# Four pairs of k tiles in three more units of a Strassen-like matmul kernel, and results added to memory by DMA

## The chip, the cores and the metric

The kernel runs on one core of a Trainium2 chip. A core has a matrix engine (PE, with its weight load PEld), a vector engine (DVE), a scalar engine (ACT), a general engine (POOL) and an engine that here only issues loads (SP). Each works through its own list of instructions in order; semaphores make one wait for another. DMA queues move data beside them. The metric is the device time of one execution in microseconds (us), as the median of several; smaller is better.

## The reference

The input is one sequence of 256 tokens with 2048 channels in float32, and one layer of a residual network is computed:

```python
u = rms_norm(h, norm_mix_w)
z = u @ w_in                                  # 2048 x 11264
...
gate_a, gate_b = jnp.split(jax.nn.sigmoid(gates), 2, axis=-1)
merged = gate_a * (y_a @ w_branch_a) + gate_b * (y_b @ w_branch_b)
h = h + merged @ w_out
u = rms_norm(h, norm_mlp_w)
h = h + jnp.square(jax.nn.relu(u @ w_up)) @ w_down      # 2048 -> 8192 -> 2048
return rms_norm(h, norm_final_w)
```

y_a comes from a gated linear recurrence (8 heads) and y_b from banded attention (16 heads) over parts of z. The change concerns the last columns of `u @ w_in`, which are the two gates, and the last part of `@ w_down` together with the final norm.

## The kernel before, in words

**Products.** Each float32 operand is split into a high part (rounded to fp32r) and a low part (what is left), by an ACT cast and a DVE subtraction (`split`, L88 to L90). A product of one tile of 128 k rows is three matmuls: high by high, high by low, low by high (`mm3`, L142 to L145).

**Units.** From the second half of the first gate on, the work is cut into units (`gemm_s`, L718 to L888). A unit makes 256 tokens by 1024 columns from 16 k tiles: two token blocks m = 0, 1 by two column blocks n = 0, 1 of 512. Of its 16 k tiles, r pairs (k, k + 4) are treated as 2 by 2 blocks in the manner of Strassen and Winograd: seven products for eight, with sums of weight blocks (`add`, L740 to L742, on DVE), sums of activation blocks (S2, S4, S5 and S7, made by `combos`, L615 to L646) and four running sums in PSUM that take copies of each other (`copy`, L770 to L773, on ACT) and are combined there (`more`, L775 to L777, on DVE). The other k tiles are plain products (`plain`). A unit has 192 − 3r matmuls of 128x512. With r = 3 the third pair is in mixed tiles X and Y, whose 256 KB halves are loaded one by one, and the k tiles 3 and 7 in another mixed pair `r0_3`, `r1_3`; with r = 4 all loads are whole 512 KB tiles.

The products are named p1, p3, p5, p2, p6, p7, p4 in the order of work, with px, py, px2 for the mixed tiles, and the plain pairs r0_k and r1_k. Product p7 goes into the sum c21 after ACT has copied that sum out (u1); u2 is the copy after p7.

The units in order: ga2 (second half of the first gate), gb0 and gb2 (second gate), then eight plain products with the branch weights, wo0 and wo2 (w_out), and four quarters of the MLP. A quarter has two w_up units and two w_down units, which are named up00, up02, dn00, dn02 in quarter 0, and so on to dn30 and dn32. All have r = 3 but wo2 and one w_up unit (r = 2) and the w_down units of quarters 0 to 2 (r = 4).

The last plain pair of a unit's second column block, with the hand-over of its results, is kept back as a closure (`late`) and issued within the next unit by `flush` (L892): with r = 4 before p5 (L794 to L797), with r = 3 after p2 (L809).

**Results.** A unit calls `done` or `out_of` per result of 128x512. Gates go through a sigmoid on ACT. For w_down, `out_of` (L1015 to L1039) has two ways. In quarters 0 to 2, ACT copies the PSUM sum to a token tile y (L1020) and POOL issues a DMA that adds it to the residual tile h in SBUF (L1021). In the last quarter DVE adds the sum to h directly (`evict`, L714 to L716); then ACT squares the tile for the final norm (`ysq`, L1024) and DVE multiplies it by the norm's weights `wf` (L1026). When n = 3 is done, the norm is finished and the output is written.

**Activations of a quarter.** `turn` (L973 to L985) transposes squared ReLU results on PE, ACT copies the blocks needed for the sums, and ACT and DVE split them; `turns` (L990 to L996) calls `combos` on them. `pairs` (L988) is 3 in the last quarter and 4 in the others. With four pairs `combos` makes the fourth entry of its sums in tiles of their own, S5m and S2m. The sums for x (Sx) are made once, before the gates, with three entries.

**Buffers and order.** Weights pass through rings of buffers: raw 6 + 2, high parts 4 + 2, low parts 4 + 2 (`BUFS`, `buf`, `piece`, `parts`, L662 to L699). A load is issued when DVE's split has released its raw buffer. PSUM has six banks for sums (`ps_k`). Token tiles of 128x512 share 17 buffers. The order of instructions on each engine is set by a scheduler, which goes by the program's order and by the priority that `tc.high_priority` raises.

Of the kernel before, what the change touches and what calls it, by code (L numbers as in the profile page):

```python
# [8 lines left out]
F32 = mybir.dt.float32  # L9
# [7 lines left out]
P = 128  # L17
T = 256
NM = T // P
D = 2048  # L20
KD = D // P
FF = 8192
NC = 512
# [27 lines left out]
def tile_hybrid_block(  # L51
# [5 lines left out]
    nc = tc.nc  # L57
    x, out = x[0], out[0]
# [29 lines left out]
    def split(hi, lo, src, copy=None):  # L88
        (copy or nc.scalar.copy)(hi, src)  # L89
        nc.vector.tensor_tensor(lo, src, hi.bitcast(F32), op=ALU.subtract)  # L90
# [7 lines left out]
    def new_act(what):  # L98

        return apool.tile([P, 4, 2, T], F32R, name=f"act_{what}", tag="act")  # L100
# [49 lines left out]
    def gemm(lhs, w, n0, nkt, what, wide=False, between=None):  # L150

        acc = new_acc(what)
        for kt, wh, wl in weights(w, n0, nkt, NC, what, wide=wide):
            if between and between[0][0] == kt:
                between.pop(0)[1]()
            for m in range(NM):
                mm3(acc[:, m, :], *lhs_of(lhs, kt, m), wh, wl, kt == 0, kt == nkt - 1)
        return acc
# [33 lines left out]
    xT = [new_act(f"x{c}") for c in range(4)]  # L192
# [14 lines left out]
    done = [0, 0]  # L207
    for kt, n in zip(starts, steps):
        c, a = kt // 4, kt % 4
# [290 lines left out]
    a, sc, vs, gws, ends = [None] * 4, [[] for _ in range(4)], [None] * 2, [None] * 2, []  # L500
# [28 lines left out]
    tk = ctx.enter_context(tc.tile_pool(name="tokens", bufs=1, reuse_waits="tile"))  # L529
# [6 lines left out]
    TOK = 17  # L536
# [49 lines left out]
    for g in range(2):  # L586
        qT = [qk_chunk(C_AQ + g * NC + i * T, f"aq{g}{i}", rstd8_t, None if g or i else acc_q0) for i in range(2)]
        kT = [qk_chunk(C_AK + g * NC + i * T, f"ak{g}{i}", rstd_t) for i in range(2)]
        acc = gemm(xT, w_in_n, C_AV + g * NC, KD, f"av{g}")
# [7 lines left out]
        for pr in range(5):  # L597
            last = pts
# [5 lines left out]
    def token(what):  # L604
        return tk.tile([P, NC], F32, name=what, tag="t", bufs=TOK)


    def sigmoid(gate, acc, m):
        with tc.high_priority(offset=2000):
            nc.scalar.activation(gate, acc, AF.Sigmoid, scale=rstd[:, m:m + 1])  # L610
        return gate

    R = 3

    def combos(lhs, what, home, blocks=None, n=R):  # L615

        a = blocks
        if not a:
            a = []
            for m in range(NM):  # L620
                for j in range(2):
                    t = tk.tile([P, R, P], F32, name=f"a{m}{j}_{what}", tag="t", bufs=TOK)
                    x = lhs[j][:, :R, :, m * P:(m + 1) * P].bitcast(F32)
                    nc.vector.tensor_tensor(t, x[:, :, 0, :], x[:, :, 1, :], op=ALU.add)
                    a.append(t)
        a11, a12, a21, a22 = a
        s5 = a22
        nc.vector.tensor_tensor(s5, a21, a22, op=ALU.subtract)
        s7 = a21
        nc.vector.tensor_tensor(s7, a11, a21, op=ALU.subtract)  # L630
        s2 = a11
        nc.vector.tensor_tensor(s2, s5, a11, op=ALU.subtract)
        s4 = a12
        nc.vector.tensor_tensor(s4, a12, s2, op=ALU.add)
        made = {}
        for two in ((5, s5), (4, s4)), ((2, s2), (7, s7)):
            if n > R:
                more = tk.tile([P, 2, 2, P], F32R, name=f"S{two[0][0]}m_{what}", tag="t", bufs=TOK)
            for q, (i, s) in enumerate(two):
                t = (tk if home == "a" else xp).tile([P, R, 2, P], F32R, name=f"S{i}_{what}", tag=f"S{i}{home}", bufs=1)  # L640
                split(t[:, :, 0, :], t[:, :, 1, :], s[:, :R])
                made[i] = [[t[:, k, u, :] for u in range(2)] for k in range(R)]
                if n > R:
                    split(more[:, q, 0, :], more[:, q, 1, :], s[:, R])
                    made[i].append([more[:, q, u, :] for u in range(2)])
        return made  # L646

    Sx = combos(xT, "x", "a")
    ga, gb = [], []
    for n in range(2):  # L650
        acc = gemm(xT, w_in_t, C_GA + n * NC, KD, f"ga{n}", wide=True)
# [62 lines left out]
    def evict(dst, acc):  # L714
        with tc.high_priority(offset=2000):
            nc.vector.tensor_tensor(dst, acc, dst, op=ALU.add)  # L716
# [175 lines left out]
    def flush():  # L892

        while late:
            late.pop()()

    for gates, c, col, what, fresh in ((ga, 2, C_GA, "ga", True), (gb, 0, C_GB, "gb", True), (gb, 2, C_GB, "gb", False)):
        gates += [[None] * NM for _ in range(2)]

        def done(m, n, acc, gates=gates, c=c, what=what):  # L900
            gates[c + n][m] = sigmoid(token(f"gate_{what}{c + n}{m}"), acc, m)

        gemm_s(xT, Sx, w_in_t, col + c * NC, f"{what}{c}", done, fresh=fresh)
    flush()


# [9 lines left out]
    for n in range(4):  # L916
        for y, w, gate, what in ((ya, w_branch_a, ga[n], "ba"), (yb, w_branch_b, gb[n], "bb")):
            acc = gemm2(y, w, n * NC, 8, f"{what}{n}")
# [35 lines left out]
    for n0 in (0, 2):  # L954
        for n in (n0, n0 + 1):
            for m in range(NM):
                t = token(f"h1_{n}_{m}")
# [10 lines left out]
    for qd in range(NQ):  # L968
        last = qd == NQ - 1
        uT = []  # L970
        pend = []

        def turn(ahead=0):  # L973

            c, rs = pend.pop(0)
            uT.append(new_act(f"u{qd}{c}"))
            hi, lo = uT[-1][:, :, 0, :], uT[-1][:, :, 1, :]
            for m in range(NM):
                tp = transpose4(rs[m], f"u{qd}{c}{m}")
                if c < 2:  # L980
                    blocks[m, c] = tk.tile([P, pairs, P], F32, name=f"a{m}{c}_u{qd}", tag="t", bufs=TOK)
                    nc.scalar.copy(blocks[m, c], tp[:, :pairs])
                with tc.high_priority(offset=ahead):
                    split(hi[:, :, m * P:(m + 1) * P], lo[:, :, m * P:(m + 1) * P], tp)

        Su = {}
        blocks = {}
        pairs = R if last else 4  # L988

        def turns():  # L990
            if len(hT) == 2:
                h_blocks(2)
            while pend:
                turn()
            if len(uT) == 2:
                Su.update(combos(uT, f"u{qd}", "b", [blocks[m, j] for m in range(NM) for j in range(2)], pairs))  # L996

        for c in range(0, 4, 2):
            rs = {}

            def done(m, n, acc, c=c, rs=rs):
                t = token(f"r{qd}{c}")
                with tc.high_priority(offset=2000):
                    nc.scalar.activation(t, acc, AF.Relu, scale=rstd2[:, m:m + 1])
                nc.scalar.activation(t, t, AF.Square)
                rs[m, n] = t
                if m == NM - 1:
                    pend.append((c + n, [rs[i, n] for i in range(NM)]))

            gemm_s(hT, Sh, w_up, qd * (FF // NQ) + c * NC, f"up{qd}{c}", done, r=R if qd or c else 2, between=turns)  # L1010
        if last:
            wf = apool.tile([P, D], F32, name="wf", tag="act")
            nc.gpsimd.dma_start(wf, bass.AP(tensor=norm_final_w.tensor, offset=norm_final_w.offset, ap=[[0, P], [1, D]]))

        def out_of(m, n, acc, last=last):  # L1015
            r = h1[n][m]
            if not last:
                t = token(f"y{qd}{n}{m}")
                with tc.high_priority(offset=2000):
                    nc.scalar.copy(t, acc)  # L1020
                nc.gpsimd.dma_start(r, t, accum_op=ALU.add)  # L1021
                return
            evict(r, acc)
            nc.scalar.activation(token(f"ysq_{n}_{m}"), r, AF.Square, accum_out=ssq3[:, m, n:n + 1])  # L1024
            if n < 3:
                nc.vector.tensor_tensor(r, r, wf[:, n * NC:(n + 1) * NC], op=ALU.mult)  # L1026
                return
            nc.vector.tensor_reduce(ssum3[:, m:m + 1], ssq3[:, m, :], axis=AX.X, op=ALU.add)
            rsqrt(rstd3[:, m:m + 1], ssum3[:, m:m + 1], D, 1)
            f = rstd3[:, m:m + 1]  # L1030
            for i in range(4):
                t = h1[i][m]
                if i == 3:
                    nc.vector.scalar_tensor_tensor(t, t, f, wf[:, i * NC:(i + 1) * NC], op0=ALU.mult, op1=ALU.mult)
                elif i == 2:
                    nc.vector.tensor_scalar(t, t, f, None, op0=ALU.mult)
                else:
                    nc.scalar.activation(t, t, AF.Copy, scale=f)
                (nc.sync if i % 2 else nc.scalar).dma_start(out[m * P:(m + 1) * P, i * NC:(i + 1) * NC], t)  # L1039

        for n0 in (0, 2):
            gemm_s(uT, Su, w_down, n0 * NC, f"dn{qd}{n0}", lambda m, n, acc, n0=n0: out_of(m, n0 + n, acc), r=pairs, kt0=qd * KD,
                   front=None if n0 else lambda: turn(2000), between=None if n0 else turns, tail=last and n0 == 2)


# [42 lines left out]
```

## Time and profile before

| | |
|---|---|
| median of 3 runs | 1408.56 us (1408.13 to 1408.87) |
| the profiled execution | 1410.16 us, its span 1408.4 us |
| mean granted clock of PE | 0.998 of full speed |
| matrix engine busy | 99% |
| vector engine busy | 82% |
| scalar engine busy | 63% |

The page of the profile gives the busy time per engine, the span in 40 slices, the chain of work that ended last, the costliest groups of instructions and the DMA issues. Times in the timeline are us from the start of the span: a row has the start, the duration, the engine, the line of the kernel, the operation, what it writes and reads, the shape, and in brackets the idle time before it with what ended that. A matmul's row is longer than its place in the pipeline, so the distance from one start to the next is what counts. A row of the windows has a stretch, its length, the busy time of PE, PEld, DVE, ACT and POOL with the number of their instructions, the granted clock, the busy share of the DMA engines and GB/s.

### The profile page before, as it was taken

To read this page: it belongs to the slowest core of one execution; us is meant where nothing else is said; L and a number is where in the kernel's file an instruction comes from. 1 tells how busy PE (TensorE), PEld (TensorE's weight loads), DVE (VectorE), ACT (ScalarE), POOL (GpSimd) and SP (SyncE) were. 2 spreads that over 40 slices of the span, in tenths; PEclk is the share of its full clock that TensorE was granted. 3 is DMA by queue.
4 is the path that set the end of the run, shared out by engine and by line. 5 is a ranking of instruction groups with operands and counts; after the bars stand their busy time and mean duration, and the time that the engine had idled before them with its cause. 6 is when DMAs were issued, how large, how long until landed. Compare 5 with 4: busy or idle time off the path is not lost.

```text
span 1408.4 us, 18482 instructions
## 1 busy us (share of the span) xinstructions
PE 1393.6 (99%) x6611; PEld 1158.0 (82%) x6611; DVE 1150.2 (82%) x1484; ACT 888.1 (63%) x1191; POOL 54.8 (4%) x116
## 2 busy tenths in 40 slices
PE   9999999999999999999999999999999999999997
PEld 7889888878787888888888888888888888888885
DVE  7798987575767784688998889879997899978984
ACT  6867745363655664345666776668666776667753
POOL 3000001010000000000000000000000000000000
PEclk9999999999999999999999999999999999999999
DMA  9654545555456756656654567754678547777542
GB/s 313 241 178 139 180 147 163 191 166 179 155 179 210 239 192 214 213 174 225 210 192 138 182 235 236 227 209 150 220 244 269 187 131 230 232 267 239 188 149 98
DMA packets 122157, 279.13 MB, mean 198 GB/s; under 512 B 10192, under 2 KB 31440, under 8 KB 121680
## 3 DMA queue, kind: packets, MB, share of 16 engines
q1 hardware_dynamic: 115872, 264.80, 56.2%
q0 software_dynamic: 5040, 11.54, 3.9%
q10 hardware_dynamic: 1152, 1.60, 0.3%
q8 instruction: 52, 0.85, 0.2%
q14 instruction: 41, 0.34, 0.1%
HBM read 269.51 MB, written 2.10 MB: 193 GB/s over the span
## 4 chain that ended last, share of the span: by engine, by line
PE 92%; DVE 3%; DMA 2%; issue 1%; ACT 1%; POOL 0%; SPq 0%; POOLq 0%; ACTq 0%; DVEq 0%
PE acc_ak L175 2%; PE acc_aq L175 2%; DMA raw_hf<-in_w_in_t_dram 1%; PE ps L393 1%; PE acc_hf L175 1%; PE acc_ga L144 1%; PE acc_hg L145 1%; PE acc_hg L143 1%; PE acc_bb L145 1%; PE acc_bb L143 1%; PE acc_ga L145 1%; PE acc_ga L143 1%; PE acc_hg L144 1%; PE acc_ba L145 1%; PE acc_av L144 1%
## 5 line engine op out<-in xcount | busy, mean ns | idle before, releaser
L742 DVE TENSOR_TENSOR raw_dn<-raw_dn,raw_dn 128x1024 f32<-128x1024 f32 x56 | 67.8, 1219 | 0.4
L175 PE MATMUL acc_hf<-act_x,wh_hf 128*128 128x512 f32 x128 | 45.8, 396 | 0.7 <-DVE wh_hf L89 0.6
L175 PE MATMUL acc_aq<-act_x,wh_aq 128*128 128x512 f32 x128 | 46.5, 401 | 0.0
L175 PE MATMUL acc_hq<-act_x,wh_hq 128*128 128x512 f32 x128 | 45.6, 395 | 0.0
L175 PE MATMUL acc_ak<-act_x,wh_ak 128*128 128x512 f32 x128 | 45.0, 397 | 0.0
L742 DVE TENSOR_TENSOR raw_up<-raw_up,raw_up 128x1024 f32<-128x1024 f32 x32 | 39.1, 1223 | 0.7
L1021 POOL DMA_DIRECT2D h<-y x24 | 20.5, 865 | 471.5 <-ACT y L1020 470.7
L174 PE MATMUL acc_aq<-act_x,wl_aq 128*128 128x256 f32 x120 | 34.6, 288 | 0.0
L174 PE MATMUL acc_hf<-act_x,wl_hf 128*128 128x256 f32 x120 | 34.2, 285 | 0.2 <-DVE wl_hf L90 0.2
L90 DVE TENSOR_TENSOR wl_av<-raw_av,wh_av 128x1024 fp32r<-128x1024 f32 x16 | 19.6, 1224 | 18.1 <-ACT wh_av L89 18.1
L174 PE MATMUL acc_hq<-act_x,wl_hq 128*128 128x256 f32 x120 | 34.0, 283 | 0.0
L174 PE MATMUL acc_ak<-act_x,wl_ak 128*128 128x256 f32 x120 | 33.6, 280 | 0.0
L90 DVE TENSOR_TENSOR wl_ba<-raw_ba,wh_ba 128x1024 fp32r<-128x1024 f32 x16 | 19.6, 1224 | 16.6 <-ACT wh_ba L89 16.6
L89 ACT CAST wh_ba<-raw_ba 128x1024 fp32r<-128x1024 f32 x16 | 16.9, 1053 | 24.3 <-PE acc_ba L145 10.0
L90 DVE TENSOR_TENSOR wl_bb<-raw_bb,wh_bb 128x1024 fp32r<-128x1024 f32 x16 | 19.6, 1222 | 14.7 <-ACT wh_bb L89 14.7
L90 DVE TENSOR_TENSOR wl_aq<-raw_aq,wh_aq 128x1024 fp32r<-128x1024 f32 x16 | 19.6, 1225 | 14.3 <-ACT wh_aq L89 14.2
L89 ACT CAST wh_bb<-raw_bb 128x1024 fp32r<-128x1024 f32 x16 | 16.9, 1054 | 22.8 <-PE acc_ba L145 12.7
L90 DVE TENSOR_TENSOR wl_ga<-raw_ga,wh_ga 128x1024 fp32r<-128x1024 f32 x16 | 19.6, 1224 | 13.8 <-ACT wh_ga L89 13.8
L89 ACT CAST wh_aq<-raw_aq 128x1024 fp32r<-128x1024 f32 x16 | 16.8, 1047 | 22.2 <-PE acc_hg L145 10.9
L89 ACT CAST wh_av<-raw_av 128x1024 fp32r<-128x1024 f32 x16 | 16.8, 1052 | 22.0 <-PE acc_av L145 12.4
L89 ACT CAST wh_hg<-raw_hg 128x1024 fp32r<-128x1024 f32 x16 | 16.7, 1045 | 20.7 <-PE acc_hg L145 9.7
L175 PEld LDWEIGHTS acc_hf<-act_x,wh_hf 128*128 128x128 f32 x128 | 24.0, 188 | 6.2 <-DVE wh_hf L89 0.8
(1470 smaller groups left out, 5136.1 us busy)
## 6 DMA issues: line engine op xcount, KB each, us to landing
raw_dn<-in_w_down_dram SPq DMA_DIRECT2D x56, 512.0 KB, 5.8
raw_up<-in_w_up_dram SPq DMA_DIRECT2D x32, 512.0 KB, 6.8
raw_ga<-in_w_in_t_dram SPq DMA_DIRECT2D x20, 512.0 KB, 4.4
raw_hi<-in_w_in_n_dram SPq DMA_DIRECT2D x16, 512.0 KB, 4.2
raw_hg<-in_w_in_n_dram SPq DMA_DIRECT2D x16, 512.0 KB, 3.6
raw_aq<-in_w_in_t_dram SPq DMA_DIRECT2D x16, 512.0 KB, 4.1
raw_ak<-in_w_in_t_dram SPq DMA_DIRECT2D x16, 512.0 KB, 3.7
raw_av<-in_w_in_n_dram SPq DMA_DIRECT2D x16, 512.0 KB, 4.3
```

Source lines behind the costliest of these rows:

```text
L89: (copy or nc.scalar.copy)(hi, src)
L90: nc.vector.tensor_tensor(lo, src, hi.bitcast(F32), op=ALU.subtract)
L143: nc.tensor.matmul(acc, hi, wh, start=first, stop=False, skip_group_check=True)
L144: nc.tensor.matmul(acc, hi, wl, start=False, stop=False, skip_group_check=True)
L145: nc.tensor.matmul(acc, lo, wh, start=False, stop=last, skip_group_check=True)
L174: nc.tensor.matmul(acc[:, cb, 0:T], wl[:, c], r[:, 0, :], start=False, stop=False)
L175: nc.tensor.matmul(acc[:, cb, :], wh[:, c], r.rearrange("p u t -> p (u t)"), start=kt == 0, stop=kt == nkt - 1)
L393: nc.tensor.matmul(ps[:, m, :], klf[:, a * P:(a + 1) * P], qrf[:, a * 192:(a + 1) * 192], start=True, stop=True)
L742: nc.vector.tensor_tensor(dst, dst, t, op=ALU.add)
L1021: nc.gpsimd.dma_start(r, t, accum_op=ALU.add)
```

## The change

Four pairs of k tiles instead of three are used in gb0, gb2 and dn30. For the gates, `combos` gets a range of k tiles, and a second call makes the fourth entry of the sums for x. In the last quarter, blocks and sums are made for four pairs as in the others. dn32 stays at three pairs. The results of dn30 (n = 0, 1) are copied by ACT and added to h by a POOL DMA, as in the other quarters; the squares and the multiplication by wf stay behind them. Those of dn32 are still added by DVE.

```diff
-    def combos(lhs, what, home, blocks=None, n=R):
+    def combos(lhs, what, home, blocks=None, n=R, ks=slice(0, R)):
+        nk = ks.stop - ks.start
...
-                    t = tk.tile([P, R, P], F32, name=f"a{m}{j}_{what}", tag="t", bufs=TOK)
-                    x = lhs[j][:, :R, :, m * P:(m + 1) * P].bitcast(F32)
+                    t = tk.tile([P, nk, P], F32, name=f"a{m}{j}_{what}", tag="t", bufs=TOK)
+                    x = lhs[j][:, ks, :, m * P:(m + 1) * P].bitcast(F32)
...
-                split(t[:, :, 0, :], t[:, :, 1, :], s[:, :R])
-                made[i] = [[t[:, k, u, :] for u in range(2)] for k in range(R)]
+                split(t[:, :nk, 0, :], t[:, :nk, 1, :], s[:, :nk])
+                made[i] = [[t[:, k, u, :] for u in range(2)] for k in range(nk)]
...
+    for i, s in combos(xT, "x3", "b", ks=slice(R, 4)).items():
+        Sx[i] += s
     for gates, c, col, what, fresh in ((ga, 2, C_GA, "ga", True), (gb, 0, C_GB, "gb", True), (gb, 2, C_GB, "gb", False)):
...
-        gemm_s(xT, Sx, w_in_t, col + c * NC, f"{what}{c}", done, fresh=fresh)
+        gemm_s(xT, Sx, w_in_t, col + c * NC, f"{what}{c}", done, r=R if what == "ga" else 4, fresh=fresh)
...
-                    blocks[m, c] = tk.tile([P, pairs, P], F32, name=f"a{m}{c}_u{qd}", tag="t", bufs=TOK)
-                    nc.scalar.copy(blocks[m, c], tp[:, :pairs])
+                    blocks[m, c] = tk.tile([P, 4, P], F32, name=f"a{m}{c}_u{qd}", tag="t", bufs=TOK)
+                    nc.scalar.copy(blocks[m, c], tp)
...
-        pairs = R if last else 4
...
-                Su.update(combos(uT, f"u{qd}", "b", [blocks[m, j] for m in range(NM) for j in range(2)], pairs))
+                Su.update(combos(uT, f"u{qd}", "b", [blocks[m, j] for m in range(NM) for j in range(2)], 4))
...
         def out_of(m, n, acc, last=last):
             r = h1[n][m]
-            if not last:
+            if last and n > 1:
+                evict(r, acc)
+            else:
                 t = token(f"y{qd}{n}{m}")
                 with tc.high_priority(offset=2000):
                     nc.scalar.copy(t, acc)
                 nc.gpsimd.dma_start(r, t, accum_op=ALU.add)
+            if not last:
                 return
-            evict(r, acc)
...
-            gemm_s(uT, Su, w_down, n0 * NC, f"dn{qd}{n0}", lambda m, n, acc, n0=n0: out_of(m, n0 + n, acc), r=pairs, kt0=qd * KD,
+            gemm_s(uT, Su, w_down, n0 * NC, f"dn{qd}{n0}", lambda m, n, acc, n0=n0: out_of(m, n0 + n, acc), r=R if last and n0 else 4, kt0=qd * KD,
```

## The prediction

> **What bounds the kernel now.** I read the page's head and its chain of waits first, then windows over whole units, then the timeline at the places that the change touches.
>
> ```profile
> span 1408.4 us, 18482 instructions
> PE 1393.6 (99%) x6611; PEld 1158.0 (82%) x6611; DVE 1150.2 (82%) x1484; ACT 888.1 (63%) x1191; POOL 54.8 (4%) x116
> PE 92%; DVE 3%; DMA 2%; issue 1%; ACT 1%; POOL 0%; SPq 0%; POOLq 0%; ACTq 0%; DVEq 0%
> ```
>
> PE is busy for 99% of the span and is 92% of the chain. A matmul taken away is therefore worth its pitch, and a wait that reaches PE costs its whole length. The windows (us, PE, PEld, DVE, ACT, POOL busy, PEclk, DMA share, GB/s) are of a gate unit with three pairs and of a w_down unit that already has four pairs and DMA adds:
>
> ```profile
> 460.00:501.00 41.00, 41.00 (x182) 33.95 (x182) 32.89 (x32) 25.49 (x29) 0.00 (x0) 1.00 0.62 205
> 1017.00:1058.00 41.00, 41.00 (x182) 33.94 (x182) 38.17 (x36) 26.43 (x30) 2.89 (x4) 1.00 0.76 232
> ```
>
> **The change part by part.** *Fewer matmuls.* A unit has 192 − 3r matmuls, so r = 4 instead of 3 in gb0, gb2 and dn30 removes 3 × 3 = 9; the built kernels differ by just these (6197 and 6188 PE rows).
>
> ```profile
> 421.50 0.39 PE L143 MATMUL acc_ga2c<-wh_ga2p,S_x 128*128 128x512 f32 x1
> 423.54 0.39 PE L143 MATMUL acc_ga2c<-wh_ga2p,S_x 128*128 128x512 f32 x1
> ```
>
> These two are nine matmuls apart in an unbroken stretch: −2.04 us, 0.227 each.
>
> *The extra combinations in ga2.* The fourth pair's sums for x are 12 DVE operations of 128x128 (four adds, four combinations, four low parts) and four ACT casts. In the built order nine of the 12 stand ahead of ga2's px2 split (at 426.33 before), seven of them in the idle time before 421.66 or pushing what follows.
>
> ```profile
> 421.66 1.22 DVE L90 TENSOR_TENSOR wl_ga2p<-raw_ga,wh_ga2p 128x1024 fp32r<-128x1024 f32 x1 [1.22 <-PE acc_ga2c L786]
> 426.33 1.22 DVE L90 TENSOR_TENSOR wl_ga2px<-raw_ga2x,wh_ga2px 128x1024 fp32r<-128x1024 f32 x1
> 427.58 1.40 SPq L680 DMA_DIRECT2D raw_ga2r<-in_w_in_t_dram  x1
> 435.80 2.00 ACT L89 CAST wh_ga2r<-raw_ga2r 128x1024 fp32r<-128x1024 f32 x2 [5.35 <-DMA raw_ga2r<-in_w_in_t_dram]
> 437.70 0.58 ACT L772 COPY u_ga<-acc_ga2c 128x512 f32<-128x512 f32 x1
> 438.33 0.50 PE L143 MATMUL acc_ga2c<-wh_ga2p,act_x 128*128 128x512 f32 x1 [1.03 <-ACT u_ga L772]
> 796.24 0.28 DVE L90 TENSOR_TENSOR S5m_u<-a_u,S5m_u 128x128 fp32r<-128x128 f32 x1
> ```
>
> The only PE stall after 419 us is here. DVE's splits release the raw buffers, SP issues the loads, the last of these lands at 435.8, ACT casts it, and only then does ACT's queue reach the u copy for which PE waits 1.03 us. A 128x128 operation takes 0.21 to 0.28 us; nine at 0.23 are 2.07, of which DVE's idle 1.22 at 421.66 takes up its share: the splits, so the load and the stall, come 0.85 us later. Ends: 0 (the loads overlap what is lost) and 1.5 (little of the idle serves): **+0.85**.
>
> *Four pairs in gb0 and gb2.* Each unit gains two whole adds and one and a half splits on DVE and as many casts on ACT; the 256 KB halves of the mixed tile become whole 512 KB loads, so SP issues fewer DMAs.
>
> ```profile
> L742 DVE TENSOR_TENSOR raw_dn<-raw_dn,raw_dn 128x1024 f32<-128x1024 f32 x56 | 67.8, 1219 | 0.4
> ```
>
> At 1.22 us each this is +4.3 us of DVE, 32.9 to 37.2 of 41. The w_down unit above works at 38.17 of 41 with PE busy for all 41, and the new units have its PE order: cost 0, covered by DVE's remaining 3.8 us. Without that cover each unit would be late by what exceeds 41. ACT, at 25.5 of 41, has room for three more operations. The same holds for dn30, whose wider blocks (128x512 for 128x384) are those of the three quarters before; its chain of combinations ends where theirs does. Token buffers (17) and the x3 tiles' own buffers are free when the first quarter's pattern repeats and when mT's combinations come, two stages later.
>
> *The DMA add, and what waits for it.* dn30's four evictions move from DVE to an ACT copy (L1020) and a POOL DMA (L1021). In the other quarters nothing reads h for many microseconds after it; here a Square on ACT (ysq, for the norm) and a DVE multiplication by wf read each tile at once, so both wait for a landing. Both engines work in order. The built ACT order through the next unit, dn32, is (number, line, operation, out<-in; buffer numbers at the names' ends):
>
> ```
> 1086 L1024 TensorCopy y_11943<-acc_dn30c_11625 128x512
> 1087 L89 TensorCopy wh_dn32p_12025<-raw_dn_11982 128x1024
> 1088 L89 TensorCopy wh_dn32py<-raw_dn32y 128x1024
> 1089 L1028 Activation ysq_0_11946,ssq_6520<-h_0_0_5792 128x512
> 1090 L1024 TensorCopy y_11949<-acc_dn30c_11642 128x512
> 1091 L89 TensorCopy wh_dn32p_12051<-raw_dn_11987 128x1024
> ...
> 1094 L1028 Activation ysq_1_11952,ssq_6520<-h_0_1_5794 128x512
> ...
> 1101 L1024 TensorCopy y_12078<-acc_dn30c_11648 128x512
> 1102 L89 TensorCopy wh_dn32p_12165<-raw_dn_11987 128x1024
> 1103 L89 TensorCopy wh_dn32p4y<-raw_dn32y 128x512
> 1104 L1028 Activation ysq_0_12081,ssq_6520<-h_1_0_5796 128x512
> 1105 L1024 TensorCopy y_12084<-acc_dn30c_11710 128x512
> 1106 L89 TensorCopy wh_dn32r_3_12186<-raw_dn32r_3_12183 128x1024
> 1107 L1028 Activation ysq_1_12087,ssq_6520<-h_1_1_5798 128x512
> 1108 L773 TensorCopy u_dn_12108<-acc_dn32c_12007 128x512
> ```
>
> Each Square waits for the landing of the copy before it; the last copy (1108) is u1, for which PE's product p7 waits. Copies stand behind waits for earlier landings, so the four landings follow one another. On DVE each multiplication by wf comes behind its Square (it overwrites what that reads), with splits behind it; the splits of p7's tiles stand ahead of the last three, so p7's path is ACT's. Before, the u copy came right behind two Squares of evicted tiles. The rows for the chain, with T0 the unit's first matmul (1354.73 before):
>
> ```profile
> 1354.73 0.39 PE L143 MATMUL acc_dn32c<-wh_dn32p,act_u 128*128 128x512 f32 x1
> 1358.37 1.06 ACT L89 CAST wh_dn32p<-raw_dn 128x1024 fp32r<-128x1024 f32 x1 [0.17 <-ACT acc_dn32c L772]
> 1359.33 1.05 ACT L89 CAST wh_dn32px<-raw_dn32x 128x1024 fp32r<-128x1024 f32 x1
> 1361.33 0.57 ACT L772 COPY s_dn<-acc_dn32c 128x512 f32<-128x512 f32 x1
> 1361.80 1.05 ACT L89 CAST wh_dn32p<-raw_dn 128x1024 fp32r<-128x1024 f32 x1
> 1366.93 0.63 ACT L1024 ACTIVATE ysq<-h 128x512 f32<-128x512 f32 x1
> 1370.37 0.39 PE L143 MATMUL acc_dn32c<-wh_dn32p,S_u 128*128 128x512 f32 x1
> 1013.61 0.59 ACT L1020 COPY y<-acc_dn10c 128x512 f32<-128x512 f32 x1 [0.30 <-PE acc_dn10c L145]
> 1014.49 0.85 POOL L1021 DMA_DIRECT2D h<-y  x1 [111.68 <-ACT y L1020]
> ```
>
> Landing times, all 24 such DMAs first, then one at 1057.7 us and one at 1070.3, and the DMA share around those two and around the place in dn32:
>
> ```profile
> L1021 POOL DMA_DIRECT2D h<-y x24: 840/849/1173, 846.2 to 1238.5; - x24
> DMA to landing us min/median/max: 3.2/4.1/8.9
> ...
> L1021 POOL DMA_DIRECT2D h<-y x1: 849/849/849, 1057.7 to 1057.7; - x1
> DMA to landing us min/median/max: 4.8/4.8/4.8
> ...
> L1021 POOL DMA_DIRECT2D h<-y x1: 847/847/847, 1070.3 to 1070.3; - x1
> DMA to landing us min/median/max: 8.5/8.5/8.5
> ```
>
> ```profile
> 1057.00:1061.00 4.00, 4.00 (x19) 3.32 (x18) 3.77 (x5) 3.47 (x5) 0.85 (x1) 1.00 0.78 150
> 1068.00:1072.00 4.00, 4.00 (x19) 3.30 (x19) 3.05 (x3) 3.21 (x5) 1.70 (x2) 1.00 0.97 283
> 1366.00:1370.00 4.00, 4.00 (x19) 3.30 (x19) 4.00 (x6) 2.71 (x6) 0.00 (x0) 1.00 0.80 248
> 1370.00:1374.00 4.00, 4.00 (x20) 3.30 (x19) 2.77 (x5) 2.01 (x3) 0.00 (x0) 1.00 0.87 249
> ```
>
> The first copy starts at T0 − 3.9, as in quarter 1 (1013.61 against its unit's start at 1017.5); POOL issues 0.88 later, and the landing, at the minimum of 3.2 since the queues are quiet at a unit's start, is at T0 + 0.2. ACT comes to the first Square after two casts, at T0 + 1.0, and to the second copy 0.64 later; 0.88 and a landing of 3.3 put the second Square at T0 + 5.8. Behind it stand five casts at 0.95 from start to start (1358.37 to 1359.33) and a copy, 0.47 (1361.33 to 1361.80): with the Square 5.9, so y(1,0) starts at T0 + 11.75. Landing 3 follows 0.88 + L3 behind that, then 0.64 for the Square, 0.88 + L4, 0.64, and 0.5 for the u copy: PE may start p7 at T0 + 15.3 + L3 + L4. PE gets there at T0 + 17.2: 15.64 as before plus the 7 matmuls (1.59) that the new PE order puts ahead of it. The idle time is L3 + L4 − 1.9. For L3 and L4 I take 4.8 each, because their share, 0.80 to 0.87, is nearest to 0.78: **+7.7 us**, ends 4.5 (3.2 each) and 15.1 (8.5 each). Behind p7 PE finds its tiles ready, and the tail is unchanged. ACT, DVE and SP are late together, but PE's stall gives all of them that time.
>
> *The clock after such a stall.*
>
> ```profile
> 1399.00:1403.00 4.00, 0.14 (x1) 0.00 (x0) 2.15 (x5) 2.05 (x4) 0.55 (x1) 1.00 0.72 262
> 1403.00:1408.00 5.00, 0.00 (x0) 0.00 (x0) 0.00 (x0) 0.00 (x1) 0.00 (x0) 0.54 0.57 211
> 1.10:4.00 2.90, 2.88 (x13) 2.89 (x14) 0.67 (x1) 1.28 (x1) 2.86 (x13) 1.00 0.67 154
> 4.00:5.40 1.40, 1.40 (x13) 1.22 (x11) 0.68 (x3) 0.00 (x0) 1.40 (x6) 1.00 0.84 207
> ```
>
> After its last matmul (1399.14) the granted clock falls about 4.3 us later, and at the start 13 small matmuls took 2.88 us and the next 13 took 1.40. So an idle time over 4.3 us is followed by some 2.9 us at half speed: **+1.4 us**, ends 0 and 1.7. The Trainium skill ("TensorE: Matmul & The Clock Gate", "What's actually happening") puts both the idle window and the recovery at about 3.4 us; by that rule the loss would be 1.7 us, and the trace's 4.3 and 2.9 lie on either side of it.
>
> *Sum*: −2.04 + 0.85 + 7.7 + 1.4 = +7.9. The profiled execution took 1410.16 us (span 1408.4) and would take 1418.1; the median of the runs is 1408.56, so **1416.5**.
>
> **The rivals.** *The landings stay hidden* (the other side). If POOL's DMAs landed sooner than ACT comes to the Squares, only the matmuls would count: −2.04, 1406.5, no change that can be told; were ga2's 1.03 us stall to vanish also, −3.07, 1405.5, faster. It decides where L3 + L4 is under 1.9 us; the shortest of 24 is 3.2. Or ACT might meet the Squares later than I lay out, which would move them behind the landings. *Short landings*: at 3.2 each and with no loss of clock, −2.04 + 0.85 + 4.5 = +3.3, 1411.9. For it speaks that half of the 24 are under 4.1, against it the share of 0.80 and more. The Trainium skill ("DMA: Bandwidth & Descriptors", "Anatomy of one DMA — SWDGE (gpsimd) path") fits 2.0 us and bytes over 436 GB/s, an estimate of 2.6 us for these 256 KB; by it the idle time would be 3.3, the time 1410.7; no row here is so short. *DVE overloaded*: if each of the three new units had a stall like ga2's 1.03 us, with the landings hidden, −2.04 + 0.85 + 3.1 = +1.9, 1410.5; the unit at 38.17 without one speaks against it.
>
> **How the numbers follow.** About 0.2% (2.8 us) can be told from no change. The forecast with its long landings has 0.60; short landings 0.20 (0.04 of it within 0.2%); DVE overload 0.04 (half within); hidden landings 0.16 (half faster, half within). So faster 0.08, same 0.04 + 0.02 + 0.08 = 0.14, slower 0.78. The range leaves out the hidden case and the last of the long one. Below: −2.04, no delay in ga2, 4.5 of idle and full clock are +2.5, 1411.0, and with the DVE case 1410.5. Above: the extreme, −2.04 + 1.5 + 15.1 + 1.7 = +16.3, would be 1424.8; both landings at 8.5 I hold unlikely and stop at 1422.5.
>
> **What the changed kernel's profile would show.** Right: in the waits of PE a stall of 5 to 15 us in dn32 before p7, released by ACT's u copy; four ACT Squares idle on h<-y DMAs one after another; the clock under 1 behind it; a stall of about 1.9 us in ga2; no new wait in gb0, gb2 or dn30. Wrong: the Squares without idle time ahead of them; landings under 3 us; DVE as the releaser in gb0 or gb2.

## The result and the profile after

| | median | runs | profiled execution, its span |
|---|---|---|---|
| before | 1408.71 us | 6, from 1407.64 to 1409.52 | 1410.16 us, 1408.4 |
| changed | 1418.53 us | 6, from 1416.64 to 1419.58 | 1416.64 us, 1414.8 |

The ratio is 1.0069, with a 95% interval from 1.0059 to 1.008: slower by 9.8 us. The profiled execution of the changed kernel is the shortest of its six, and its span is only 6.4 us above that of before. From the start of a unit's first matmul to that of the next unit's, both in the timelines, the time went here (us):

| | ga2 | gb0 | gb2 and the branches | dn30 | dn32, to PE's last end |
|---|---|---|---|---|---|
| before | 40.36 | 41.71 | 134.02 | 43.38 | 44.41 |
| changed | 39.63 | 41.02 | 133.26 | 42.59 | 55.22 |

The three units with fewer matmuls are each shorter by 0.7 to 0.8 us (three matmuls are 0.68). One unit, dn32, whose own products did not change, is longer by 10.8 us. What is left between the two spans, −1.4 us, lies almost all ahead of ga2 and behind PE's last matmul, outside these units. The longest waits of PE in the changed kernel (waited for, us in total, times, longest) are both there, and the third line is ga2's:

```profile
PE acc_dn32c L143 <- ACT wh_dn32r L89: 5.2, 1, 5.2
PE acc_dn32c L143 <- ACT u_dn L773: 3.0, 1, 3.0
...
PE acc_ga2c L143 <- DVE acc_ga2c L778: 0.3, 1, 0.3
```

ACT's timeline in dn32 shows what held it. The unit's first matmul is at 1350.88.

```profile
1347.00 0.59 ACT L1024 COPY y<-acc_dn30c 128x512 f32<-128x512 f32 x1 [3.02 <-PE acc_dn30c L145]
...
1351.10 0.63 ACT L1028 ACTIVATE ysq<-h 128x512 f32<-128x512 f32 x1 [0.67 <-DMA h<-y]
...
1356.05 0.64 ACT L1028 ACTIVATE ysq<-h 128x512 f32<-128x512 f32 x1 [1.36 <-DMA h<-y]
...
1361.89 0.59 ACT L1024 COPY y<-acc_dn30c 128x512 f32<-128x512 f32 x1
...
1371.08 0.63 ACT L1028 ACTIVATE ysq<-h 128x512 f32<-128x512 f32 x1 [7.13 <-DMA h<-y]
...
1371.70 0.56 ACT L1024 COPY y<-acc_dn30c 128x512 f32<-128x512 f32 x1
1372.17 1.04 ACT L89 CAST wh_dn32r<-raw_dn32r 128x1024 fp32r<-128x1024 f32 x1
1375.77 0.63 ACT L1028 ACTIVATE ysq<-h 128x512 f32<-128x512 f32 x1 [2.56 <-DMA h<-y]
...
1376.40 0.57 ACT L773 COPY u_dn<-acc_dn32c 128x512 f32<-128x512 f32 x1
```

Each of the four Squares waits for the landing of the DMA add before it (0.67, 1.36, 7.13 and 2.56 us). The fourth copy to y (1371.70) and the cast of r0_3 (1372.17) stand behind the third Square, the u copy behind the fourth. PE's timeline answers:

```profile
1367.65 0.39 PE L145 MATMUL acc_dn32c<-wh_dn32r,act_u 128*128 128x512 f32 x1
1373.27 0.80 PE L143 MATMUL acc_dn32c<-wh_dn32r,act_u 128*128 128x512 f32 x1 [5.23 <-ACT wh_dn32r L89]
1377.02 0.80 PE L143 MATMUL acc_dn32c<-wh_dn32p,S_u 128*128 128x512 f32 x1 [2.95 <-ACT u_dn L773]
1377.61 0.63 PE L144 MATMUL acc_dn32c<-wl_dn32p,S_u 128*128 128x512 f32 x1
...
1380.96 0.39 PE L143 MATMUL acc_dn32c<-wh_dn32r,act_u 128*128 128x512 f32 x1
```

The one matmul at 1373.27 is the first of r0_3, which this order puts ahead of p7 (1377.02). The two waits add up to 8.2 us. Counted from start to start, since the rows of matmuls overlap, 9.37 us pass from 1367.65 to 1377.02 where two matmuls take 0.45: p7 is late by 8.9. Behind that the nine matmuls from 1377.02 to 1380.96 take 3.94 us where nine take 2.04 at full clock: 1.9 us. 8.9 and 1.9 make up dn32's 10.8. The single matmul ran slowly too (0.80 us), but behind it PE waited for the u copy in any case; the expectations below count it with the clock, at 2.5 us in all. The windows (us, PE, PEld, DVE, ACT, POOL busy, PEclk, DMA share, GB/s) show the clock and the queues in this time:

```profile
1363.00:1367.00 4.00, 4.00 (x20) 3.30 (x19) 3.56 (x5) 0.94 (x2) 0.62 (x1) 1.00 0.92 228
1367.00:1371.00 4.00, 1.04 (x5) 0.54 (x3) 0.00 (x0) 0.00 (x0) 0.00 (x0) 0.96 1.03 325
1370.50:1371.00 0.50, 0.00 (x0) 0.00 (x0) 0.00 (x0) 0.00 (x0) 0.00 (x0) 0.64 1.01 410
...
1373.00:1377.00 4.00, 0.80 (x1) 0.29 (x1) 1.70 (x2) 1.41 (x4) 0.41 (x1) 0.50 0.47 109
1377.00:1380.00 3.00, 2.98 (x7) 2.40 (x8) 0.83 (x2) 0.02 (x1) 0.00 (x0) 0.50 0.00 0
1380.50:1381.00 0.50, 0.50 (x3) 0.36 (x3) 0.00 (x0) 0.50 (x1) 0.00 (x0) 0.62 0.00 0
```

From the two short windows, the clock went to half at about 1370.6, which is 2.6 us after the last matmul ended (1367.65 and 0.39), and back at about 1380.8: 10.1 us at half.

The third and the fourth add, each with its time to landing:

```profile
L1025 POOL DMA_DIRECT2D h<-y x1: 847/847/847, 1362.8 to 1362.8; - x1
...
DMA to landing us min/median/max: 8.3/8.3/8.3
...
L1025 POOL DMA_DIRECT2D h<-y x1: 842/842/842, 1372.6 to 1372.6; - x1
...
DMA to landing us min/median/max: 3.2/3.2/3.2
```

The third went into full queues, with shares of 0.92 and 1.03, and took 8.3 us. The fourth took 3.2: by then the raw buffers were full, DVE could release none, and the loads were running out (share 0.47 from 1373 to 1377). The stall quieted the queues for the last landing; in the version without a stall, below, the fourth add took 9.2 us.

### The profile page after: what moved, and what is told of

Its sections match the earlier page's. It is cut to its first block, busy times and chain, and to the rows that moved or that the text cites. A ratio compares the mean times of both kernels' runs of the same rounds, so it can differ in the third digit from the quotient of the medians.

```text
span 1414.8 us, 18497 instructions
## 1 busy us (share of the span) xinstructions
PE 1394.0 (99%) x6602; PEld 1158.6 (82%) x6602; DVE 1161.8 (82%) x1499; ACT 896.0 (63%) x1206; POOL 58.3 (4%) x120
## 4 chain that ended last, share of the span: by engine, by line
issue 52%; PE 38%; DVE 4%; POOL 2%; DMA 1%; ACT 1%; POOLq 0%; SPq 0%; ACTq 0%; DVEq 0%
PE acc_ak L175 2%; PE acc_aq L175 2%; PE acc_hf L175 2%; POOL h L1025 2%; PE acc_hq L175 1%; PE ps L393 1%; PE acc_hg L145 1%; PE acc_hg L143 1%; PE acc_hg L144 1%; PE acc_av L144 1%; PE acc_av L143 1%; PE acc_av L145 1%; PE acc_aq L174 1%; PE acc_ak L174 1%; PE acc_gb2c L143 1%
## 5 line engine op out<-in xcount | busy, mean ns | idle before, releaser
L743 DVE TENSOR_TENSOR raw_dn<-raw_dn,raw_dn 128x1024 f32<-128x1024 f32 x60 | 72.5, 1219 | 0.4
L1025 POOL DMA_DIRECT2D h<-y x28 | 23.9, 866 | 604.6 <-ACT y L1024 603.7
L175 PEld LDWEIGHTS acc_aq<-act_x,wh_aq 128*128 128x128 f32 x128 | 24.1, 188 | 5.6 <-issue 0.7
```

Source lines behind the costliest of these rows:

```text
L175: nc.tensor.matmul(acc[:, cb, :], wh[:, c], r.rearrange("p u t -> p (u t)"), start=kt == 0, stop=kt == nkt - 1)
L743: nc.vector.tensor_tensor(dst, dst, t, op=ALU.add)
```

## The experiments

The theory: the time is that of landings 3 and 4, met in ACT's order ahead of r0_3's cast and the u copy, and of the clock behind them. Its main rival: the fourth pairs' additional work on DVE, or the DMA adds as such.

**DVE evictions instead of the DMA adds, four pairs kept.**

```diff
-            if last and n > 1:
+            if last:
                 evict(r, acc)
```

> Four pairs everywhere as in the changed kernel, but all results of the last quarter are added to h by DVE. Theory (the landings, met one after another in ACT's queue, cost the time): no stall in dn32, so before's 1408.7 us less nine matmuls (2.04), and less up to 0.7 for ga2, whose stall was 0.3 us in the changed kernel's profile for 1.03: 1406.0 to 1406.7. Rival (DVE's additional sums for r = 4 cost the time): the 9.8 us stay for the most part, 1414 or more.

Measured: 1406.64 us (11 runs, ratio to before 0.9986, from 0.9977 to 0.9995), with no wait of PE in dn32. The adds cost 11.9 us, and the rest of the change saves 2.0 (before had 1408.62 beside this run).

**The DMA adds alone, three pairs.**

```diff
-            if not last:
+            if last and n > 1:
+                evict(r, acc)
+            else:
                 ...
-            evict(r, acc)
```

> The kernel before with the DMA add for n = 0 and 1 of the last quarter alone; three pairs in all its units. Theory: the stall in dn32 is as in the changed kernel, some 8 us of idle time and 2.5 us at half clock, and the matmuls are those of before: 1408.7 + 10.8 = 1419.5, between 1416 and 1421 as the landings fall. Rival (the fourth pairs cost the time): 1408.7.

Measured: 1418.52 us (ratio 1.0075, from 1.0062 to 1.0087). The first line of PE's waits:

```profile
PE acc_dn32c L143 <- ACT u_dn L772: 8.3, 1, 8.3
```

With no fourth pair added anywhere, a wait of 8.3 us appears, near the 8.2 of the changed kernel and in one piece (here r0_3 does not stand ahead of p7). The fourth pairs are not the cause.

**All four DMA adds kept, the Squares issued later.**

```diff
+            if n < 2:
+                held_back.append((m, n))
+                return
+            while held_back:
+                i, k = held_back.pop(0)
+                ...            # Square and multiplication by wf of h1[k][i]
```

> The changed kernel, its four DMA adds kept, but the four Squares and multiplications by wf of n = 0 and 1 are issued when the results of n = 2 are handed over, behind dn32's u copies in ACT's order. Theory: nothing is queued behind a landing, so the stall goes, 1406.0 to 1406.7. Rival (the DMA adds cost by their traffic or by ACT's copies, wherever the Squares stand): 1412 or more.

Measured: 1406.68 us (11 runs, ratio 0.9987, from 0.9978 to 0.9996). ACT's timeline has the third and fourth copies and the u copy close together, and the first Square behind the second u copy, with no idle time ahead of it:

```profile
1361.76 0.59 ACT L1026 COPY y<-acc_dn30c 128x512 f32<-128x512 f32 x1 [0.30 <-PE acc_dn30c L145]
1363.12 0.59 ACT L1026 COPY y<-acc_dn30c 128x512 f32<-128x512 f32 x1 [0.77 <-PE acc_dn30c L145]
...
1365.16 0.59 ACT L773 COPY u_dn<-acc_dn32c 128x512 f32<-128x512 f32 x1
1370.20 0.57 ACT L773 COPY u_dn<-acc_dn32c 128x512 f32<-128x512 f32 x1
1371.62 0.62 ACT L1035 ACTIVATE ysq<-h 128x512 f32<-128x512 f32 x1
```

The fourth add now runs beside the loads and takes long to land, but nothing waits for it:

```profile
L1027 POOL DMA_DIRECT2D h<-y x1: 840/840/840, 1364.0 to 1364.0; - x1
...
DMA to landing us min/median/max: 9.2/9.2/9.2
```

The DMA adds cost nothing that can be measured; where the instructions that need their result stand in an in-order queue costs 11.9 us. The run moves DVE's multiplications together with the Squares; that the queue was ACT's is read from what released PE in the changed kernel, not tested apart. This version and the one with evictions are the best of the study, both below the kernel before by 2 us, and neither faster than the other.

**Only n = 1 by DMA, and only n = 0.** In the changed kernel `n > 1` becomes `n != 1`, and in the other `n > 0`.

> The changed kernel with n = 0 of the last quarter added by DVE and only n = 1 by DMA. Theory: landings 1 and 2 cost nothing, 3 and 4 all; the third copy can start about 1.2 us earlier, when PE has finished its sum: 1417.3, between 1413 and 1418.5 as landing 3 falls. Rival (all four landings carry the cost, in equal shares): half of the 11.8 us between 1406.7 and 1418.5 goes, 1412.6.

> The changed kernel with only n = 0 of the last quarter added by DMA and n = 1 by DVE. Theory: ACT waits about 2 us in all for landings 1 and 2, while PE has work ahead, so PE has no stall in dn32: 1406.0 to 1406.7. Rival (all four landings carry the cost): 1412.6.

Measured: 1417.53 us (ratio 1.0064, from 1.005 to 1.0078) and 1407.55 us (ratio 0.9993, from 0.9984 to 1.0002). Landings 3 and 4 carry all of it but about a microsecond. The second time is 0.9 us above the range that was expected. PE's waits with n = 1 alone by DMA:

```profile
PE acc_dn32c L143 <- ACT u_dn L773: 4.6, 1, 4.6
PE acc_dn32c L143 <- ACT wh_dn32r L89: 2.9, 1, 2.9
```

With n = 0 alone there is a small wait in dn32 that was expected to be nothing, and ga2's, which in this execution was 1.0 us:

```profile
PE acc_ga2c L143 <- DVE acc_ga2c L778: 1.0, 1, 1.0
...
PE acc_dn32c L143 <- ACT u_dn L773: 0.7, 1, 0.7
```

**The gates' part alone**, with the last quarter as before.

> Only the gates' part of the change: the fourth entry of the sums for x, and four pairs in gb0 and gb2. Theory: six matmuls less, 1.36 us, and a stall in ga2 that the extra DVE operations move by something between -0.7 and +0.85 us: 1406.6 to 1408.2. Rival (DVE overloaded at r = 4, or ga2 delayed): 1409.5 or more.

Measured: 1407.70 us (11 runs, ratio 0.9993, from 0.9985 to 1.0002). That is 1.0 us less, with the 1.36 of six matmuls inside the interval; it can't be told from no change. gb0 takes 41.03 us in its profile, three matmuls less than before, with DVE busy for 36.7 of it, so DVE was not overloaded.

**The kernel before, profiled once more.**

> The kernel before once more, for a second profile of it. If the 1.03 us stall in ga2 is its own, it is there again at 0.9 to 1.1 us; if it hangs on how one load lands in one execution, it is another figure or gone. The time is 1408.7 either way, within 1 us.

Measured: 1409.28 us (10 runs, ratio 1.0004, from 0.9995 to 1.0014). The stall in ga2 is gone. What differs is how long that unit's r loads, issued from 424 to 432 us, took to land. First the profile that the prediction used, then the new one:

```profile
DMA to landing us min/median/max: 4.8/7.8/8.1
```

```profile
DMA to landing us min/median/max: 4.1/5.4/6.1
```

In the ten other profiles, with and without the extra sums, the median is 5.2 to 6.1. The 1.03 us were those of one execution. The span is no shorter for that, 1408.5 us: here the clock was at half from about 9.4 to 12.8 us, which the first profile does not have.

```profile
9.00:9.50 0.50, 0.35 (x2) 0.36 (x3) 0.50 (x3) 0.37 (x2) 0.50 (x2) 0.89 0.93 262
9.50:10.00 0.50, 0.50 (x4) 0.40 (x3) 0.50 (x2) 0.50 (x2) 0.50 (x4) 0.50 0.84 180
12.50:13.00 0.50, 0.50 (x3) 0.43 (x2) 0.03 (x1) 0.50 (x2) 0.00 (x0) 0.70 0.75 238
```

PE's waits shortly before it were three, of 0.2, 0.6 and 0.5 us. The nine profiled kernels with the extra sums have another wait in ga2, for DVE's addition into PSUM (L778): 0.3 us in seven of them, 0.6 and 1.0 in the others. From ga2's first matmul to gb0's they take 39.6 us in six, 39.9 in two and 40.4 in one; the two profiles with neither the sums nor the 1.03 us take 39.0 and 39.2.

**Unread matmuls where PE would wait.** In the changed kernel dn32 issues matmuls into a free PSUM tile behind r1_3, whose result nothing reads: 36, then 46. The scheduler places 34 and 44 of them straight ahead of p7.

```diff
         plains(1, left[0])
+        if tail:
+            ps = ps_tp2.tile([P, 4, P], F32, name="ps_busy", tag="tp").rearrange("p a n -> p (a n)")
+            for _ in range(36):        # 46 in the second
+                nc.tensor.matmul(ps, lhs[0][:, 0, 0, 0:P], lhs[0][:, 0].rearrange("p u t -> p (u t)"), start=True, stop=True)
```

> The changed kernel with 36 matmuls of 128x512 added in dn32 whose result nothing reads; 34 of them (7.7 us) stand in PE's order straight ahead of p7, where PE would wait, and the seven matmuls that the changed kernel does ahead of p7 come behind it. Theory with the clock: PE's wait shrinks to about 2.3 us, the granted clock stays at 1.00 behind it, which saves 2.5 us, and the seven matmuls cost 1.6: 1417.6, 0.9 less than the changed kernel. Rival (no loss by the clock): 1418.5 + 1.6 = 1420.1.

> The changed kernel with 46 unread matmuls instead of 36, of which 44 (10.0 us) stand ahead of p7: the 2.7 us for which PE still waited with 36 shrink to about 0.5. In that kernel the granted clock was 0.50 for 3.4 us behind the wait, which cost 1.6 us. Theory (PE's own idle time takes the clock down): it stays at 1.00 and the time falls to 1417.6. Rival (the drop is not due to PE's idle time): 1419.2 and the drop again.

Measured: 1419.19 us with 36 (ratio 1.0072, from 1.006 to 1.0085) and 1417.86 us with 46 (1.0067, from 1.0055 to 1.008). The first missed its number, 1417.6, and lies nearer to the rival's 1420.1: PE waited 2.74 us, near the 2.3 expected, but the clock did fall. PE's rows, and then windows of 0.6 us around them:

```profile
1378.67 0.50 PE L143 MATMUL acc_dn32c<-wh_dn32p,S_u 128*128 128x512 f32 x1 [2.74 <-ACT u_dn L773]
1379.01 0.40 PE L144 MATMUL acc_dn32c<-wl_dn32p,S_u 128*128 128x512 f32 x1
...
1380.10 0.63 PE L145 MATMUL acc_dn32c<-wh_dn32p,S_u 128*128 128x512 f32 x1
```

```profile
1379.20:1379.80 0.60, 0.60 (x4) 0.47 (x4) 0.28 (x1) 0.00 (x0) 0.00 (x0) 0.94 0.00 0
1379.80:1380.40 0.60, 0.60 (x3) 0.50 (x2) 0.00 (x0) 0.00 (x0) 0.00 (x0) 0.50 0.00 0
...
1382.80:1383.40 0.60, 0.60 (x4) 0.46 (x3) 0.27 (x1) 0.60 (x1) 0.00 (x0) 0.71 0.00 0
```

PE was at work again at 1378.67 with full clock, and a microsecond later the clock went to half for 3.4 us. The drop came after the idle time, while PE was busy. With 46 the wait and the drop are gone:

```profile
PE acc_dn32c L143 <- ACT u_dn L773: 0.2, 1, 0.2
```

```profile
1378.00:1382.00 4.00, 3.85 (x17) 3.18 (x18) 2.04 (x3) 2.26 (x4) 0.00 (x0) 1.00 0.00 0
```

With ten more useless matmuls the median is 1.3 us lower, 0.7 by the ratios, whose intervals overlap; the times alone do not show a gain, over the version with 36 or over the changed kernel (1.0069). The rows do show the clock's part: with 36, eight matmuls from 1379.71 on took 3.38 us, 1.6 more than at full clock, and with 46 none is slow.

**Four pairs in dn32 too**, with evictions throughout the last quarter (`r=4` for both w_down units).

> All results of the last quarter added by DVE, as in the run that did that, and four pairs in dn32 too: three more matmuls less, 0.68 us: 1406.0. Rival (dn32 needs its slack at the end, where ACT also has the Squares of n = 0 and 1): 1407 or more.

Measured: 1406.69 us (11 runs, ratio 0.9988, from 0.9979 to 0.9997): no gain over 1406.64, though its profiled span, 1404.7 us, is 0.7 shorter than that of the run with three pairs there (1405.4). Three matmuls are below what these runs can tell, and whether something in the tail takes them back stays open.

## Why the prediction was right

The direction, the mechanism and the place are those forecast, and 1418.53 lies in the range, 2.0 us above the 1416.5 predicted. Which steps make up these 2.0 us is not shown, since the profiled execution is 1.9 us shorter than the median; the sizes below are those of that one execution. By its steps:

- *Fewer matmuls*, −2.04: the three units lost 0.69, 0.76 (with the branches behind gb2) and 0.79 us in the profile, 2.2 in all; the run with evictions is 2.0 below before. The profiles count 6611 and 6602 PE instructions, nine apart; the 6197 and 6188 of the prediction stand in no profile.
- *ga2*, +0.85: wrong in its base and in its path. The step took a stall of one execution for a property of the kernel; the second profile of before has none. The extra sums do delay ga2, but by the wait for DVE's addition: 39.6 us in most profiles with them, against 39.0 and 39.2 without them and without the stall, which is some 0.4 to 0.6 us. Against the profile that the prediction used, ga2 came out 0.73 us shorter. That +0.85 lies near these 0.4 to 0.6 us is luck, since it was worked out from another wait.
- *Four pairs in gb0 and gb2 on DVE*, 0: right, by the table and the run with the gates alone (DVE 36.7 us busy in gb0, where 37.2 was forecast).
- *The landings*, +7.7: 8.9 in the profile, as p7's start is late. Of the terms, y(1,0) started at T0 + 11.0 for 11.75 and PE's row broke off at T0 + 17.0 for 17.2. L3 was 8.3 and L4 3.2, where 4.8 each was taken: the two terms were off in opposite directions, and that their sum was near is luck. The chain itself holds: its formula with these two landings and the earlier start of y(1,0) puts p7 at T0 + 26.05, and it started at T0 + 26.14. The DMA share that stood for both was that of the kernel before, and the wait itself changes it: without a stall, with the Squares later, these two adds took 7.9 and 9.2 us. The prediction named the u copy as the releaser; the larger part, 5.2 us, came by r0_3's cast one place ahead of it, which its working had left out.
- *The clock*, +1.4: 1.9 in the profile, above its upper end of 1.7. The length of slow work had been taken from the start of the kernel, 2.9 us, by the pace alone: the window shown there has a granted clock of 1.00. Here it was 3.7 us from p7's start on, and 3.4 in the run with 36 unread matmuls. The bound of 4.3 us of idle time, from the kernel's end, was wrong as a threshold too: in the changed kernel the clock fell 2.6 us after the last matmul, in the run with 36 a wait of 2.74 us sufficed, and in the second profile of before it fell with no wait over 0.6 us near it. At half it stayed for 3.4 us in these last two, and for 10.1 or 10.2 in the changed kernel, with the adds alone and with n = 1 alone. The Trainium skill ("TensorE: Matmul & The Clock Gate", "What's actually happening") has a window of about 3.4 us for both directions, and says that the window runs freely. These times are close to once and three times 3.4 us; that PE was already busy for a microsecond when the clock fell is in keeping with a decision made at the end of such a window, though no run here shows the window itself.

The rival of hidden landings is what two runs made true: with the Squares later, or with the evictions, the time is the 1406.5 that the prediction gave for it, to within 0.2 us. The rival of DVE overload fell with the gates' run.

## What to carry to other kernels

The DMA adds were cheap here as long as nothing needed their result soon; before moving one to a DMA, look in the built order for the first instruction that reads it, and for what stands behind that instruction on its in-order engine. Issue that reader late: the same four adds cost 11.9 us or nothing. And take a stall that the sum rests on from more than one execution, above all where a load's landing ends it.

## What was not expected of the hardware

- The granted clock fell about 1.1 us after PE had resumed from a wait of only 2.74 us, and stayed at half for 3.4 us; with ten more unread matmuls in the waiting time the wait was 0.2 us and the clock stayed at 1.00.
- It fell in one profile of the kernel before with no wait of PE over 0.6 us near it, for 3.4 us, near the kernel's start. Where PE's waits were longer it stayed at half for 10.1 to 10.2 us.
- Landing times of like adds, 256 KB each, in one place differ by what the rest of the program does to the queues: 8.3 us at a share of 0.92 to 1.03, and 3.2 us ten microseconds later, when the stall that the first had made had let the loads run dry. Without a stall the two took 7.9 and 9.2 us.
